# A new set of scheduling numbers for a two-layer decoder trunk on one NeuronCore

## The chip, the cores and the metric

The kernel runs on one core of one Trainium2 chip, in float32. The metric is the device time of one launch in microseconds (us). The engines of the core are named as in the profile: PE (matmuls; PEld its weight loads), DVE (the vector engine), ACT (the scalar engine), POOL (GpSimd) and SP (whose queue issues the DMAs here). All values are float32; products that need full precision are made of three matmuls, as described below.

## The reference

```python
for l in range(2):                                   # x: 256 tokens x 1024
    x = x + 0.5 * swiglu(rmsnorm(x, ffn1_norm[l]), ffn1_w_gate[l], ffn1_w_up[l], ffn1_w_down[l])
    h = rmsnorm(x, mix_norm[l])
    (q, kc, vc, ksl, vsl, kw, vw, gts, hq, hf, hi, hg) = split(h @ w_in[l])
    o_nsa = nsa_group(...)      # 8 heads of 64, 2 key groups: compressed, selected and window branches
    o_hg = hgrn2_group(...)     # 4 heads of 128: a gated linear recurrence in chunks of 64
    x = x + concat([o_nsa, o_hg]) @ w_out[l]
    x = x + 0.5 * swiglu(rmsnorm(x, ffn2_norm[l]), ffn2_w_gate[l], ffn2_w_up[l], ffn2_w_down[l])

def swiglu(x, w_gate, w_up, w_down):                 # w_gate, w_up: 1024 x 2816
    return (silu(x @ w_gate) * (x @ w_up)) @ w_down
```

So each layer is an FFN, a mixer (attention and recurrence side by side, one input and one output projection) and a second FFN.

## The kernel before

The 256 tokens stay in SBUF as two halves h = 0 and h = 1 of 128 rows (`X`). All weights are streamed once through the core in units of 128 x 1024 numbers: `load_stream` (L395) brings a unit into one of three raw buffers, `hi_stream` (L413, on ACT) rounds it to the high part `hi`, `lo_stream` (L432) takes the difference `lo = raw - hi` on DVE or, with `pool=True`, on POOL, and `stream(h)` (L458) multiplies: three matmuls per product, hi with the high part of the activations, lo with it, and hi with their low part (L485 to L487; `wide_unit`, L501, does the same with the weights as the moving operand at L515 to L517). The pairs hi, lo live in a ring of five slots; a raw buffer is free once `lo` is made, and a slot once both halves have used it.

The mixer's other work hangs on the blocks of the input projection, in the order q, kv, kw, hf, hq, hi, hg. `head_task` (L1166) makes the scores of two heads (matmuls L1174 and L1175), their row maxima and the exponentials; the weights of a head are then scaled by `buf<-buf,mx`, on DVE (L358) or ACT (L334). `turn_task` (L1194) transposes them, and `attend_task` (L1104) splits them into pth and ptl and multiplies with the values into the PSUM tile `po` (L1144 to L1146, L1158). `cmp_task` (L1203) does the branch of the compressed keys on tiles `pc`. The recurrence is in `level_task` (L1307): for chunks halved six times it forms `hx` from exponentials of the prefix sums `S` and `P`; `products` (L1348) multiplies these pieces on PE (L1368), `last_product` (L1378, matmul L1385) and the product `S<-S,kk` (at L1344, run by the helper `tt`, L345) close it, and `out_task` (L1400) makes the recurrence's output of each half in `po` (L1419 and L1421) and normalises it (squares on ACT into kk, sum at L1425, power on POOL, `kk<-po,ost`, which is the last reader of `po`). There is a single PSUM buffer `po`. Then the units of the output projection (`OUT_ORDER`, L1453: pairs of input part, 0 for attention and 1 for the recurrence, and output column half n) run through the same stream, `resid` (L672) adds x, `norm` (L680) normalises the rows (power on POOL at L376, scaling at L690) and `norm_turn` (L697) transposes the result for the next FFN (L382), whose stream needs it.

Nothing in this order is written out by hand. While the program is built, `Sched.run` (L212) holds all tasks that have a next operation ready to be placed, estimates for each the earliest start on each engine that may do it (`when`, L191, from the program's own cost formulas), picks the engine by the estimated end plus `BIAS` of that engine, and then the task with the smallest start plus its penalty. Penalties come from `PEN` by the name of the task, `STEP` by half or group, `PREP` for the two weight preparations by how far they are ahead, `FLOW` and `LAG` (`stream_pen`, L531) for the two streams, and `FIRST` for the first transposes. The result is one fixed list of instructions for each engine; the chip then runs each list in order, with semaphore waits between engines. Helpers that give the scheduler a choice of engine are `copy` (ACT or DVE), `tt` (DVE, and POOL where allowed) and `ts` (DVE, POOL or ACT). So the numbers set both the order and the engine.

Of the kernel before, what the change touches and what calls it, by code (L numbers as in the profile page):

```python
# [46 lines left out]
BOOT = 3  # L47

BOOT_X = ((-1, 0, 1, 2), (0, 0, 2, 4), (2, 1, 0, 2), (3, 1, 2, 4))
FIRST = (-0.3, -0.4, 0.5, 1.3, 0.1, 0.6, 0.9, 0.2)  # L50
LAG = 4
NBUF = 14
OUT_ORDER = ((0, 0), (0, 1), (1, 0), (1, 1))
POOL_LO = True
ORDER = ('q', 'kv', 'kw', 'hf', 'hq', 'hi', 'hg')

PEN = {"norm_turn": 0.1, "next_gain": 2.25, "gates_task": 0.15, "compress_task": -0.05, "level_task": 0.25,
       "boot": -1.0, "first_gain": -0.3, "first_norm": -0.25, "pad": 3.35, "hi_task": -3.8, "load_stream": 3.25,
       "done": 0.25, "kv_task": 0.65, "turn": 2.65, "load_w1": 3.15, "mix_prepare": -0.2, "c_turn": -3.3,
       "f_task": 0.25, "q_turn": 0.05, "kw_task": -6.1, "q_task": 0.6, "hg_task": 0.75, "hq_task": 0.45,  # L60
       "last_product": -0.15, "k_turn": 0.15, "products": 0.05, "turn_task": -0.1, "attend_task": -0.05,
       "out_task": 0.05, "k_task": 0.4, "cmp_task": -0.1, "first_turn": -0.65, "head_task": -0.1, "log_task": 0.15}
STEP = {'h': -0.16, 'g': 0.03, 'r': 0.0}
PREP = (-0.2, 0.25, 0.55, 0.75)
FLOW = (0.25, 0.15, 0.15)
BIAS = {'POOL': 0.1, 'ACT': -0.05}
SWITCH = 0.8


# [53 lines left out]
class Sched:  # L123
# [17 lines left out]
    def spawn(self, gen, pen=0.0, deps=(), phase=None):  # L141
        if not callable(pen):
            pen += PEN.get(gen.__name__, 0.0)
        t = Task(gen, pen, deps, phase)
# [61 lines left out]
            self.held[eng] = [x for x in mine if x[1] > low]  # L206
        self.held[eng].sort()

    def emit(self, t, eng, start, end, fn):
        fn()  # L210

    def run(self):  # L212
        while self.tasks:
            while any(not isinstance(t.req, Op) and self.resolve(t) for t in self.tasks):
                pass
            best = None
            for t in self.tasks:
                if not isinstance(t.req, Op):
                    continue
                pen = t.pen() if callable(t.pen) else t.pen  # L220
                one = None
                for eng, cost, fn, tab, port in t.req.alts:
                    start, more = self.when(t, eng, cost, port), 0.0
                    if eng == "PE" and (self.cold > 0 or start - self.free[eng] > 1.8):
                        cost *= 2
                    if tab and self.table not in tab:
                        cost, more = cost + LOAD, SWITCH
                    done = start + cost + BIAS.get(eng, 0.0)
                    if one is None or done < one[0]:
                        one = (done, start + pen + more, eng, start + cost, cost, fn, tab, port)  # L230
                if best is None or one[1] < best[0]:
                    best = (one[1], one, t)
            if best is None:
                if self.tasks:
                    raise RuntimeError("stuck: " + str([(t.gen.__name__, t.req[:2]) for t in self.tasks]))
                return
            _, (_, _, eng, end, cost, fn, tab, port), t = best
            if tab and self.table not in tab:
                self.table = tab[0]
                if tab[0] == "ln_exp":  # L240
                    self.nc.scalar.preload_act_table_set("natural_log_exp_and_others")
            self.emit(t, eng, end - cost, end, fn)
            if port:
                self.hold(eng, end - cost, end)
            if eng == "DMA":

                issued = end - cost + 0.475
                self.moved = max(issued + 0.65, self.moved) + cost
                end = self.moved + 0.87
            if eng == "PE":  # L250
                self.cold = (3.4 if end - cost - self.free[eng] > 1.8 else self.cold) - cost
            self.free[eng] = issued if eng == "DMA" else end
            t.deps = [(end, eng)]
            self.advance(t, (end, eng))
# [18 lines left out]
def wait(x):  # L273
    return ("wait", x)


def put(x):
    return ("set", x)
# [26 lines left out]
class Trunk(Sched):  # L305
# [148 lines left out]
    def prep_pen(self, which):  # L454
        lead = getattr(self, which) - max(self.at)
        return PREP[min(max(lead, 0), 3)]

# [73 lines left out]
    def stream_pen(self, h):  # L531
        p = min(self.phase_at[h], len(self.phases) - 1)
        a, b = self.phases[p]
        i, o = self.at[h], self.at[1 - h]
        if h and i >= b - LAG and o < b and p == self.phase_at[0]:
            return 2.0
        if not h and i < a + LAG and o >= a:
            return FLOW[0]
        return FLOW[1] + (FLOW[2] if i > o or (i == o and h) else 0.0)

# [320 lines left out]
    def mix(self, l):  # L861
# [69 lines left out]
        def values(h, br, src):  # L931

            c = lambda v: v[:, 2 * br + h, 64:].rearrange("p (g d) -> p g d", g=2)[:, :, :64]
            yield from self.split(c(M["vh"]), c(M["vl"]), src)
# [18 lines left out]
        def kw_task(h, ps):  # L953
# [7 lines left out]
            yield put(key("gt", h))  # L961
            sub(k_task(h), deps=self.keys[key("kr", h)], pen=STEP["h"] * h)
            sub(gates_task(h), deps=self.keys[key("gt", h)], pen=STEP["h"] * h)
            yield from values(h, 1, p3[:, 1])
# [139 lines left out]
        def attend_task(h, g):  # L1104
            for x in (("k", h), ("k", 0), ("q", h, g), ("g", h)):
                yield wait(key(*x))
            sub(cmp_task(h, g), pen=STEP["g"] * (2 * h + g))

# [15 lines left out]
            for r in range(R):  # L1124
                sub(head_task(h, g, r, part, pr, mx), deps=deps, pen=STEP["g"] * (2 * h + g) + STEP["r"] * r)
            for r in range(R):
# [6 lines left out]
            for i, (so, vi) in enumerate(tiles):  # L1133
                sub(turn_task(h, g, i, so, pr), deps=deps, pen=STEP["g"] * (2 * h + g) + STEP["r"] * i)
            for i, (so, vi) in enumerate(tiles):
# [316 lines left out]
        act = lambda h, kt: self.xact(h, kt) if kt > 3 else (M["ah", h][:, kt], M["al", h][:, kt])  # L1452
        for ni, (part, n) in enumerate(OUT_ORDER):  # L1453
            for k in (2 * part, 2 * part + 1):
                need = (lambda h, k=k: key("att", h, k)) if part == 0 else (lambda h: key("ho", h))
                first = k == 2 * part and part == OUT_ORDER[0][0]
                last = k == 2 * part + 1 and part == OUT_ORDER[-1][0]
                us.append(Unit(bs[n], 2 * k, [(wo[256 * k:256 * k + 256, 512 * n:512 * n + 512], 0)], first, last, act, need))

        def opened(pool, p):  # L1460
# [30 lines left out]
            for h in range(2):  # L1491
                for g in range(2):
                    sub(attend_task(h, g), pen=STEP["g"] * (2 * h + g))
                sub(log_task(h), pen=STEP["h"] * h)
# [8 lines left out]
    def build(self):  # L1503
# [12 lines left out]
        for h in range(2):  # L1516
            self.spawn(self.first_norm(h))
            for n in range(4):
                self.spawn(self.first_turn(h, n), pen=FIRST[4 * h + n])
        self.spawn(self.hi_stream(), pen=lambda: self.prep_pen("at_hi"))  # L1520
# [31 lines left out]
```

## Time and profile before

| | |
|---|---|
| runs | 1132.74, 1134.69 and 1187.89 us, median 1134.69 us |
| the profiled execution | 1132.6 us, of which the profile's span is 1130.8 us |
| PE | busy 1090.8 us (96%), mean granted clock 0.972 of full speed |
| DVE | busy 699.6 us (62%) |
| ACT | busy 577.1 us (51%) |
| POOL | busy 96.6 us (9%) |
| DMA | 186.16 MB, mean 165 GB/s |

The program's stages are seen in the span as follows: the first FFN up to about 208 us, the first mixer from 210 to about 392, two FFNs to 763, the second mixer from 765 to about 947, and the last FFN to the end. Busy times are sums over a stretch of the time in which an engine had an instruction running; an engine that is fully busy in a stretch sets its length, unless its clock is low there.

### The profile page before, as it was taken

Reading aid. Unit: us, or ns where it says so; the run is one execution under the profiler, and the core shown is the slowest. Engines: PE = TensorE matmul, PEld = TensorE weight load, DVE = VectorE, ACT = ScalarE, POOL = GpSimd, SP = SyncE. Lnnn points to the kernel's source line nnn. Section 1 sums busy time; section 2 is a strip of 40 time slices with the busy share of each in tenths; the row PEclk is TensorE's granted clock in tenths of the full one; section 3 lists DMA queues with packets and bytes.
Section 4 is the critical chain, followed back from the end, with each engine's and each line's share of the span. In section 5 each row is a group of like instructions: output and inputs, shape, how many; then the busy total and the mean of one; then the engine's idle time right before and its main releaser. Section 6 shows DMA issues by size and latency. Waiting matters only on the chain.

```text
span 1130.8 us, 18755 instructions
## 1 busy us (share of the span) xinstructions
PE 1090.8 (96%) x7420; PEld 975.9 (86%) x7420; DVE 699.6 (62%) x1242; ACT 577.1 (51%) x911; POOL 96.6 (9%) x124
## 2 busy tenths in 40 slices
PE   6999999999889999999999999999997899999998
PEld 4999988898668799998889999888975788999986
DVE  5665544689985755554465555448898857555543
ACT  6544444467664554443454444435866645444432
POOL 3100000041121100000010000001403201000000
PEclk9999999999879999999999999999998699999999
DMA  7666666565501476666666666556544125666553
GB/s 223 209 197 172 189 185 188 161 174 168 169 20 38 149 207 185 186 185 187 188 179 195 187 179 187 185 168 187 165 137 131 38 75 168 196 180 186 185 160 120
DMA packets 154168, 186.16 MB, mean 165 GB/s; under 512 B 7568, under 2 KB 117984, under 8 KB 154080
## 3 DMA queue, kind: packets, MB, share of 16 engines
q1 hardware_dynamic: 154080, 184.96, 55.1%
q8 instruction: 58, 0.95, 0.3%
q14 instruction: 30, 0.25, 0.1%
HBM read 183.89 MB, written 1.05 MB: 164 GB/s over the span
## 4 chain that ended last, share of the span: by engine, by line
PE 85%; DVE 9%; DMA 2%; issue 2%; ACT 1%; POOL 1%; SPq 0%; DVEq 0%; ACTq 0%; POOLq 0%
PE acc L515 15%; PE acc L516 15%; PE acc L517 15%; PE acc L485 11%; PE acc L487 11%; PE acc L486 11%; PE short L382 2%; DVE lo L347 2%; DVE buf L1178 1%; PE short L1368 1%; DVE xn L690 1%; DMA lg<-in_hgrn_lb_logits_dram 1%; DVE hx L347 1%; PE po L1146 1%; DVE buf L358 1%
## 5 line engine op out<-in xcount | busy, mean ns | idle before, releaser
L347 DVE TENSOR_TENSOR lo<-raw,hi 128x1024 fp32r<-128x1024 f32 (+2 forms) x329 | 394.9, 1202 | 287.2 <-ACT hi L334 286.0
L334 ACT ACTIVATE hi<-raw 128x1024 fp32r<-128x1024 f32 (+2 forms) x337 | 351.6, 1045 | 317.4 <-PE acc L487 108.0
L515 PE MATMUL acc<-xh,hi 128*128 128x256 f32 x1408 | 399.2, 284 | 0.0
L517 PE MATMUL acc<-xh,lo 128*128 128x256 f32 x1408 | 398.4, 283 | 0.0
L516 PE MATMUL acc<-xl,hi 128*128 128x256 f32 x1408 | 398.4, 283 | 0.0
L515 PEld LDWEIGHTS acc<-xh,hi 128*128 128x128 f32 x1408 | 270.2, 192 | 0.2
L516 PEld LDWEIGHTS acc<-xl,hi 128*128 128x128 f32 x1408 | 270.3, 192 | 0.1
L517 PEld LDWEIGHTS acc<-xh,lo 128*128 128x128 f32 x1408 | 270.2, 192 | 0.0
L485 PE MATMUL acc<-hi,th 128*128 128x512 f32 x352 | 139.7, 397 | 0.0
L486 PE MATMUL acc<-lo,th 128*128 128x512 f32 x352 | 139.2, 395 | 0.0
L487 PE MATMUL acc<-hi,tl 128*128 128x512 f32 x352 | 139.2, 395 | 0.0
L485 PE MATMUL acc<-hi,xh 128*128 128x512 f32 (+1 forms) x240 | 95.8, 399 | 0.0
L487 PE MATMUL acc<-hi,xl 128*128 128x512 f32 (+1 forms) x240 | 91.7, 382 | 0.0
L486 PE MATMUL acc<-lo,xh 128*128 128x512 f32 (+1 forms) x240 | 91.2, 380 | 0.0
L487 PEld LDWEIGHTS acc<-hi,tl 128*128 128x128 f32 x352 | 66.1, 188 | 16.1
L486 PEld LDWEIGHTS acc<-lo,th 128*128 128x128 f32 x352 | 66.2, 188 | 15.5
L485 PEld LDWEIGHTS acc<-hi,th 128*128 128x128 f32 x352 | 66.2, 188 | 15.5
L334 ACT ACTIVATE sg<-acc 128x512 f32<-128x512 f32 (+1 forms) x46 | 26.2, 570 | 72.0 <-PE acc L517 68.8
L376 POOL TENSOR_TENSOR rs<-rs,half 128x1 f32<-128x1 f32 x12 | 7.0, 587 | 572.6 <-DVE rs L683 572.6
L487 PEld LDWEIGHTS acc<-hi,xl 128*128 128x128 f32 x240 | 45.4, 189 | 9.1 <-DVE xl L347 0.4
L485 PEld LDWEIGHTS acc<-hi,xh 128*128 128x128 f32 x240 | 45.5, 190 | 7.8
L486 PEld LDWEIGHTS acc<-lo,xh 128*128 128x128 f32 x240 | 45.5, 190 | 6.9
(230 smaller groups left out, 1100.1 us busy)
## 6 DMA issues: line engine op xcount, KB each, us to landing
raw<-in_ffn_w_down_dram SPq DMA_DIRECT2D x88, 512.0 KB, 4.2
raw<-in_ffn_w_gate_dram SPq DMA_DIRECT2D x80, 512.0 KB, 3.8
raw<-in_ffn_w_up_dram SPq DMA_DIRECT2D x80, 512.0 KB, 3.9
raw<-in_w_in_dram SPq DMA_DIRECT2D x48, 512.0 KB, 3.8
raw<-in_w_out_dram SPq DMA_DIRECT2D x16, 512.0 KB, 3.7
buf<-in_cmp_w_dram SPq DMA_DIRECT2D x16, 256.0 KB, 7.3
raw<-in_ffn_w_gate_dram SPq DMA_DIRECT2D x13, 256.0 KB, 2.8
raw<-in_ffn_w_up_dram SPq DMA_DIRECT2D x13, 256.0 KB, 3.1
```

The costliest lines, as they stand in the source:

```text
L334: return ("ACT", c, lambda: self.nc.scalar.activation(out, in_, func, **k), TABLES.get(func), False)
L347: alts = [("DVE", 0.065 + 0.00104 * n, lambda: self.nc.vector.tensor_tensor(out, a, b, op), None, not in_psum(a) and not in_psum(b))]
L358: lambda: self.nc.vector.tensor_scalar(out, a, s1, s2, **k), None, not in_psum(a))]
L382: self.nc.tensor.transpose(o, i, self.ident[:i.shape[0], :i.shape[0]])
L485: f(ps[:, :k.n], ah, hi[:, t, :k.n], start=st, stop=False)
L486: f(ps[:, :k.n], ah, lo[:, t, :k.n], start=False, stop=False)
L487: f(ps[:, :k.n], al, hi[:, t, :k.n], start=False, stop=sp)
L515: f(ps[:, c], hi[:, t, j], xh, start=u.first and c == t == 0, stop=False)
L516: f(ps[:, c], hi[:, t, j], xl, start=False, stop=False)
L517: f(ps[:, c], lo[:, t, j], xh, start=False, stop=u.last and c == 1 and t == 3)
L690: toks.append((yield self.V(576, lambda: nc.vector.scalar_tensor_tensor(self.XN[h][:, c], self.X[h][:, c], rs[:, 0:1], self.gains[0][:, c] ...
L1146: f(po[:, :256], vh[:, vi, o:o + 128], tl[:, c], start=False, stop=False)
```

## The change

Only numbers are changed; the instructions that a task may ask for and all arithmetic stay. `emit`, an indirection around `fn()`, is taken out, so that from line 212 on a line stands three lower in the changed file. The core of the diff:

```diff
-FIRST = (-0.3, -0.4, 0.5, 1.3, 0.1, 0.6, 0.9, 0.2)
-LAG = 4
+FIRST = (-1.05, -1.18, 0.54, 0.89, 0.86, 0.63, 0.87, 0.46)
+LAG = 5
 NBUF = 14
-OUT_ORDER = ((0, 0), (0, 1), (1, 0), (1, 1))
+OUT_ORDER = ((0, 0), (0, 1), (1, 1), (1, 0))
...
-       "last_product": -0.15, "k_turn": 0.15, "products": 0.05, "turn_task": -0.1, "attend_task": -0.05,
-       "out_task": 0.05, "k_task": 0.4, "cmp_task": -0.1, "first_turn": -0.65, "head_task": -0.1, "log_task": 0.15}
-STEP = {'h': -0.16, 'g': 0.03, 'r': 0.0}
-PREP = (-0.2, 0.25, 0.55, 0.75)
-FLOW = (0.25, 0.15, 0.15)
-BIAS = {'POOL': 0.1, 'ACT': -0.05}
...
+       "k_turn": 0.16, "products": 0.15, "turn_task": -0.1, "attend_task": -0.03, "out_task": 0.06, "k_task": 0.42,
+       "cmp_task": -0.1, "first_turn": -0.74, "head_task": -0.1, "log_task": 0.16}
+STEP = {'h': -0.45, 'g': 0.03, 'r': 0.0}
+PREP = (-0.17, 0.21, 0.56, 0.75)
+FLOW = (0.16, 0.28, 0.46)
+BIAS = {'POOL': 0.07, 'ACT': -0.49}
```

`BIAS` is added to an operation's estimated end when the engine is chosen: ACT now takes one unless DVE would end more than 0.49 us earlier (0.05 before). `STEP['h']` is the lead that the second half's recurrence has over the first's, `FLOW` the penalty of the weight streams (the last number falls on the stream that is ahead of the other), and `OUT_ORDER` now leaves the column half n = 0 for the end.

In the order of the program this shows at many places of each mixer and at the start of the kernel; the FFNs' order in their steady part is the same as before. Three places follow.

The first is PE in the middle of the first mixer, where the stream has reached the third of the four hi units (`hi2`, `lo2` are ring slots, `xh` and `xl` the activations, `acc00` and `acc10` the two halves' sums). Before:

```order
L485 MATMUL acc00_63<-hi2_78,xh_84 128x512
L486 MATMUL acc00_63<-lo2_79,xh_84 128x512
L487 MATMUL acc00_63<-hi2_78,xl_85 128x512
L1368 MATMUL short1_68<-xn0_87,kk_1922 64x64 x8
...
L382 MATMUL short1_68<-ident_94,buf7_1895 128x128 x4
L485 MATMUL acc10_65<-hi2_78,xh_84 128x512
L486 MATMUL acc10_65<-lo2_79,xh_84 128x512
L487 MATMUL acc10_65<-hi2_78,xl_85 128x512
```

And now:

```order
L482 MATMUL acc00_63<-hi2_78,xh_84 128x512
L483 MATMUL acc00_63<-lo2_79,xh_84 128x512
L484 MATMUL acc00_63<-hi2_78,xl_85 128x512
L1171 MATMUL short0_67<-kh_1913,qs0_1924 128x256
L1172 MATMUL short0_67<-kl_1914,qs0_1924 128x256
L1171 MATMUL short1_68<-kh_1913,qs0_1924 128x256
L1172 MATMUL short1_68<-kl_1914,qs0_1924 128x256
...
L482 MATMUL acc10_65<-hi2_78,xh_84 128x512
```

Before, the recurrence's products (L1368) stood between the stream's matmuls and the heads' scores (L1174) came after all stream units of the input projection; now the first half's scores stand between the stream's matmuls, and the products (now L1365) come later, among the attention's transposes and value products.

The second is the end of the same mixer on PE, from the last value product of the compressed branch (`pct1`, `vcb`) on. Before (`acc00<-hi3,xh` is a unit of the output projection's part 1):

```order
L1158 MATMUL po_70<-pct1_1911,vcb_104 128x128 x2
L485 MATMUL acc00_63<-hi3_80,xh_84 128x512
...
L1419 MATMUL po_70<-xn1_91,S_1924 128x128
L1421 MATMUL po_70<-xn1_91,xn0_87 128x128
...
L485 MATMUL acc10_65<-hi0_74,ah1_1934 128x512
```

And now:

```order
L1155 MATMUL po_70<-pct1_1908,vcb_104 128x128 x2
L1365 MATMUL short1_68<-hx2_1901 64x32 x8
L1365 MATMUL short2_69<-hx0_1899 64x32 x8
L482 MATMUL acc00_63<-hi0_74,ah0_1922 128x512
...
L1382 MATMUL short0_67<-hx3_1902 64x64 x4
...
L1416 MATMUL po_70<-xn1_91,P_1920 128x128 x4
L1406 MATMUL short1_68<-P_1920,S_1921 128x128 x4
...
L1416 MATMUL po_70<-xn1_91,S_1921 128x128
L1418 MATMUL po_70<-xn1_91,xn0_87 128x128
```

Before, the first half's recurrence output (its `L1419 po<-xn1,P`, earlier than this piece) was made before the second half's attention had ended; now all attention is over when the last products of the recurrence run, and the two outputs (L1416, and L1416 with L1418) follow each other with nine stream matmuls between them.

The third is POOL in the first mixer. Before:

```order
L350 TENSOR_TENSOR hx3_1905<-hx3_1905,xn0_87 128x8x32
...
L350 TENSOR_TENSOR hx2_1904<-hx2_1904,kk_1922 128x4x64
L350 TENSOR_TENSOR lo2_79<-raw1_72,hi2_78 128x1024
L350 TENSOR_TENSOR P_1923<-P_1923 128x4x64
L1391 MEMSET P_1923 64x4x64
L350 TENSOR_TENSOR G0_1933<-G0_1933,og_115 128x512
```

And now:

```order
L347 TENSOR_TENSOR P_1920<-P_1920 128x8x32
L347 TENSOR_TENSOR S_1921<-S_1921,P_1920 128x256
L347 TENSOR_TENSOR P_1920<-P_1920 128x4x64
...
L347 TENSOR_TENSOR hx0_1899<-hx0_1899,kk_1919 128x8x32
L1388 MEMSET P_1920 64x4x64
L373 TENSOR_TENSOR ost0_1927<-ost0_1927,half_97 128x4
L373 TENSOR_TENSOR ost1_1936<-ost1_1936,half_97 128x4
L373 TENSOR_TENSOR rs0_89<-rs0_89,half_97 128x1
L347 TENSOR_TENSOR lo4_83<-raw2_73,hi4_82 128x1024
```

The unit `lo2<-raw1` in the middle of the mixer and most of the recurrence's pieces `hx` and `S` have left POOL for DVE; the unit `lo4<-raw2` behind the norm's power (`rs0`) is still on POOL, as it was before. Over the whole kernel DVE has 1213 instructions (1244 before), ACT 875 (825) and POOL 107 (126); PE has 7062 in both.

## Rows read from the trace of the kernel before

**Rows 1.** Windows: stretch, us, busy PE PEld DVE ACT POOL, PEclk, DMA share, GB/s.
```profile
60.00:200.00 140.00, 140.00 (x960) 130.00 (x960) 71.62 (x68) 61.70 (x70) 0.00 (x0) 1.00 0.63 188
260.25:345.86 85.61, 76.09 (x591) 59.37 (x590) 75.71 (x280) 57.95 (x152) 17.43 (x31) 0.84 0.37 112
265.00:297.00 32.00, 31.77 (x274) 23.90 (x273) 29.71 (x68) 19.22 (x37) 3.41 (x6) 1.00 0.47 145
297.00:350.00 53.00, 43.71 (x308) 34.60 (x307) 44.49 (x208) 37.10 (x117) 13.68 (x22) 0.74 0.26 78
345.86:377.57 31.71, 30.98 (x188) 26.66 (x187) 19.05 (x30) 14.70 (x25) 3.76 (x4) 1.00 0.24 73
815.03:900.52 85.49, 75.94 (x589) 58.66 (x587) 76.11 (x280) 58.00 (x152) 17.41 (x31) 0.84 0.36 111
```
**Rows 2.** Waits of DVE between 297 and 350: us in total, times, longest.
```profile
DVE ptl L347 <- ACT pth L334: 3.1, 4, 1.3
```
**Rows 3.** Timeline, first mixer, the recurrence's closing product: start, us, engine line operation.
```profile
345.17 0.69 DVE L347 TENSOR_TENSOR S<-S,kk 128x512 f32<-128x512 f32 x1
```
**Rows 4.** Groups by line and form, DVE and ACT: busy, mean ns, idle before.
```profile
L358 DVE TENSOR_SCALAR buf<-buf,mx 128x256 f32<-128x256 f32 x20 | 7.5, 384 | 0.0
L358 DVE TENSOR_SCALAR buf<-buf,mx 128x128 f32<-128x128 f32 x28 | 7.1, 281 | 0.0
...
L347 DVE TENSOR_TENSOR hx<-hx,kk 128x256 f32<-128x256 f32 x18 | 8.3, 458 | 0.0
L347 DVE TENSOR_TENSOR S<-S,P 128x256 f32<-128x256 f32 x20 | 8.4, 420 | 0.0
L347 DVE TENSOR_TENSOR lo<-raw,hi 128x1024 fp32r<-128x1024 f32 x315 | 385.1, 1224 | 287.2 <-ACT hi L334 286.0 <-DVE lvmask L817 0.2
L347 DVE TENSOR_TENSOR ptl<-short,pth 128x512 fp32r<-128x512 f32 x24 | 16.1, 688 | 9.9 <-ACT pth L334 9.9
...
L334 ACT ACTIVATE buf<-buf,mx 128x256 f32<-128x256 f32 x44 | 21.4, 499 | 9.9 <-DVE mx L347 7.7 <-DVE mx L358 1.7 <-POOL mx L360 0.4
```
**Rows 5.** Timeline, DVE operations beside POOL's weight splits in the first mixer.
```profile
330.89 0.23 DVE L347 TENSOR_TENSOR pc<-pc,mx 128x64 f32<-128x64 f32 x1
332.97 2.36 POOL L350 TENSOR_TENSOR lo<-raw,hi 128x1024 fp32r<-128x1024 f32 x1
333.26 2.14 DVE L347 TENSOR_TENSOR pc<-pc,mx 128x64 f32<-128x64 f32 x1
378.22 2.58 POOL L350 TENSOR_TENSOR lo<-raw,hi 128x1024 fp32r<-128x1024 f32 x1 [1.57 <-ACT hi L334]
378.48 2.86 DVE L690 SCALAR_TENSOR_TENSOR xn<-x,rs,gain 128x512 f32<-128x512 f32 x1
```
**Rows 6.** Timeline, end of the first mixer: recurrence outputs, stream matmuls, first transpose of `xn`.
```profile
350.81 0.39 PE L1419 MATMUL po<-xn,P 128*128 128x128 f32 x2
351.91 0.60 ACT L334 ACTIVATE kk<-po 128x512 f32<-128x512 f32 x1 [0.30 <-PE po L1419]
354.26 0.40 PE L487 MATMUL acc<-hi,al 128*128 128x512 f32 x1
354.57 0.69 DVE L347 TENSOR_TENSOR kk<-po,ost 128x512 f32<-128x512 f32 x1 [1.14 <-POOL ost L376]
354.96 0.39 PE L487 MATMUL acc<-hi,al 128*128 128x512 f32 x1
377.57 0.60 PE L382 MATMUL short<-ident,xn 128*128 128x128 f32 x4
```
**Rows 7.** Timeline, start of the kernel: a weight split on POOL, the norm, the first wide block.
```profile
16.78 2.40 POOL L350 TENSOR_TENSOR lo<-raw,hi 128x1024 fp32r<-128x1024 f32 x1
25.16 4.05 DVE L690 SCALAR_TENSOR_TENSOR xn<-x,rs,gain 128x512 f32<-128x512 f32 x4 [3.21 <-DMA gain<-in_ffn_norm_dram]
31.45 0.36 PE L515 MATMUL acc<-xh,hi 128*128 128x256 f32 x1
```
**Rows 8.** Windows, ten us in the middle of the mixer's attention.
```profile
320.00:330.00 10.00, 8.43 (x49) 6.68 (x51) 8.01 (x50) 8.03 (x30) 1.35 (x5) 0.54 0.01 2
```

More of the change, by code (lines that the diff above doesn't have):

```diff
@@ L49 @@
 BOOT_X = ((-1, 0, 1, 2), (0, 0, 2, 4), (2, 1, 0, 2), (3, 1, 2, 4))
-FIRST = (-0.3, -0.4, 0.5, 1.3, 0.1, 0.6, 0.9, 0.2)
-LAG = 4
+FIRST = (-1.05, -1.18, 0.54, 0.89, 0.86, 0.63, 0.87, 0.46)
+LAG = 5
 NBUF = 14
-OUT_ORDER = ((0, 0), (0, 1), (1, 0), (1, 1))
+OUT_ORDER = ((0, 0), (0, 1), (1, 1), (1, 0))
 POOL_LO = True
 ORDER = ('q', 'kv', 'kw', 'hf', 'hq', 'hi', 'hg')
[L57 to L60, printed above, removed]
-       "last_product": -0.15, "k_turn": 0.15, "products": 0.05, "turn_task": -0.1, "attend_task": -0.05,
-       "out_task": 0.05, "k_task": 0.4, "cmp_task": -0.1, "first_turn": -0.65, "head_task": -0.1, "log_task": 0.15}
-STEP = {'h': -0.16, 'g': 0.03, 'r': 0.0}
-PREP = (-0.2, 0.25, 0.55, 0.75)
-FLOW = (0.25, 0.15, 0.15)
-BIAS = {'POOL': 0.1, 'ACT': -0.05}
+PEN = {"norm_turn": 0.11, "next_gain": 1.21, "gates_task": 0.15, "compress_task": -0.05, "level_task": 0.33, "boot":
+       -1.4, "first_gain": -0.52, "first_norm": -0.26, "pad": 4.07, "hi_task": -1.73, "load_stream": 2.72, "done":
+       0.33, "kv_task": 0.75, "turn": 0.35, "load_w1": 2.96, "mix_prepare": 0.27, "c_turn": -3.76, "f_task": 0.01,
+       "q_turn": 0.26, "kw_task": -7.36, "q_task": 0.57, "hg_task": 0.73, "hq_task": 0.76, "last_product": -0.12,
+       "k_turn": 0.16, "products": 0.15, "turn_task": -0.1, "attend_task": -0.03, "out_task": 0.06, "k_task": 0.42,
[4 more added lines that the diff above has]
+BIAS = {'POOL': 0.07, 'ACT': -0.49}
 SWITCH = 0.8
@@ L207, in hold @@
         self.held[eng].sort()
-    def emit(self, t, eng, start, end, fn):
-        fn()
     def run(self):
@@ L241, in run @@
                     self.nc.scalar.preload_act_table_set("natural_log_exp_and_others")
-            self.emit(t, eng, end - cost, end, fn)
+            fn()
             if port:
```

## The prediction

> **What bounds the kernel now.** I read the windows by stage first. In an FFN's steady part PE is busy for the whole of a stretch (140 of 140 us) while DVE and ACT have half of it free [rows 1]: there the length is the matmuls' own, and since neither their number nor their order changes there, the four FFNs cost what they did. The two mixers differ. From the first mixer's last prefix sum, at 260.25, to the recurrence's closing product `S<-S,kk`, which ends at 345.86 [rows 3], DVE is busy 75.71 of 85.61 us (88.4%), PE 76.09 at a mean clock of 0.84, ACT 57.95 (68%) [rows 1]. In the first part of it (265 to 297) PE and DVE are both nearly full; from 297 to 350 no stream feeds PE, whose clock falls to 0.74, DVE has 84% and ACT 70% [rows 1]. The waits of DVE say the rest of the story there: the longest sum, 3.1 us, is for ACT's `pth` [rows 2]. So the middle of the mixer is paced by DVE, in a chain that goes back and forth between DVE, ACT and PE. Then, from 345.86 to the first transpose of the next norm at 377.57 [rows 6], PE is busy for 30.98 of 31.71 us at full clock [rows 1]: its own work sets the end. The second mixer repeats it (85.49 us, DVE 76.11) [rows 1]; I work out the first and double it.
>
> **Term 1, the middle of a mixer.** The same two points exist in the new order: the last `P<-P,S` and the product `S<-S,kk`. I count what DVE does between them, before and now, with the durations of before [rows 4].
> *Given to ACT:* the row scalings `buf<-buf,mx`, 7 of 128x256 at 0.384 and 7 of 128x128 at 0.281, together 4.66; and seven small copies of about 0.3 each (their form is nearest to the 0.281 row), 2.1. That is −6.8.
> *Taken from POOL:* five pieces `hx` at 0.458, three `S` at 0.420, one weight unit `lo` at 1.224 and one 128x512 product, which I price as the other of that size, 0.688. That is +5.5. One copy from ACT, +0.3.
> *Moved across the two ends:* the second half's attention now lies wholly ahead of the product, so six `ptl` at 0.688 and two more of 128x256 at about 0.42 come in (+5.0), while small softmax and key operations worth about 2.2 leave to the time before. That is +2.8.
> The sum is −6.8 + 5.5 + 0.3 + 2.8 = +1.8 in single durations. Neighbours on DVE overlap in the trace: 247 durations here sum to about 93.4 against 75.71 busy [rows 1], 0.07 each; there are ten instructions fewer now, so that 0.7 of overlap is lost, +2.5.
>
> Against this stands one gain that a count does not show. A DVE operation that meets a weight split on POOL lasts until the split ends: the `pc` product takes 2.14 us beside the POOL split of 2.36, and 0.23 undisturbed [rows 5], 1.9 lost; with three smaller meetings with POOL's `hx`, `S` and `P` pieces I find 4.2 us of such excess in the stretch (the smaller ones were read the same way, each against its undisturbed form). The `lo2` in the middle has left POOL, and of the recurrence's pieces few remain; I take 3.1 of the 4.2 as gone. DVE's work becomes 75.7 + 2.5 − 3.1 = 75.0 us.
>
> A rule bears on this: by the Trainium skill, "SBUF — State Buffer", section "Who interferes with whom", DVE and GpSimd share a port pair as a lock held for a whole instruction, and whoever comes second stands still. The trace agrees (2.14 against 0.23, ending with the split). It speaks against the change at one place, where `lo4` stays on POOL beside the norm's scaling.
>
> How long do 75.0 us of work take? The share of DVE in the new stretch is the open price. Bounds from rows: 93% (29.71 of 32, while ACT is at 60%) and, on the other side, 76%, which I estimate by going on from 93% at ACT 60% and 84% at ACT 70% to ACT at 79% [rows 1]. ACT takes over 14 scalings of up to 0.499 [rows 4] and the copies at about 0.36, some 9 us: 67 of about 89, 75%. I take 84%, the row in which ACT is nearest to that. 75.0 / 0.84 = 89.3, so the product ends at 349.5, 3.7 us *later* than before.
>
> **Term 2, the mixer's end.** What follows the product is shorter. Before: 377.57 − 345.86 = 31.7 us, in which value products of the second half's attention still stood. Now, on PE, with the stream's matmuls at 0.233 (0.70 for three, 354.26 to 354.96 [rows 6]): copies into `P` 1.4, the first recurrence output and the product beside it 1.8, nine stream matmuls 2.1, a wait of about 0.6 for the single `po`, the second output 1.8; then a transpose and 12 stream matmuls 3.2 with about 1.1 of waits, a transpose 0.4, and 18 + 21 stream matmuls 9.1. That is 21.4. The wait for `po` comes from the rows: from the squares' start at 351.91 to the end of `kk<-po,ost` at 355.26 are 3.35 us [rows 6], and the matmuls placed between cover the rest. What is late next is the transpose of the second half's output, queued before the last 39 matmuls; its wait is the 0.9 in the 1.1.
> The first transpose of `xn` then stands at 349.5 + 21.4 = 370.9 instead of 377.57: −6.7 a mixer. Bounds: with 93%, 340.9 + 21.4 = 362.3, −15.3; with 76%, 358.9 + 21.4 = 380.3, +2.8.
>
> **Term 3, from norm to FFN.** The scalings at L690 meet `lo4` on POOL before (2.86 against 2.58 of the split [rows 5]), and `lo4` is on POOL still. I price the passage at nothing, because both orders leave one such meeting and stream units of the next FFN stand ready on PE to cover it; without that cover it costs or saves 2.1 us a mixer (±4 for two).
> By the skill's rule above, the second to come stands still: if each passage newly held a scaling, the sum would be 4.2 us higher.
>
> **Term 4, the start.** The fourth weight unit's split goes from POOL (2.40 at 16.78) to DVE (1.22 [rows 4]). Its raw buffer comes free up to 2.1 us sooner, and behind it in SP's queue stands the DMA of the gain, for which DVE's first scalings wait 3.21 us until 25.16, and with them the first wide block at 31.45 [rows 7]. The transposes between are also regrouped. Nothing to −2.4; I take the middle, −1.2.
> Cost at nothing: the swap in `OUT_ORDER` and the order in the FFN stages, where PE is full either way.
>
> **The sum.** Against the profiled execution's 1132.6 us (span 1130.8 and 1.8 around it; the median of the runs is 2.1 higher): 1132.6 − 2 × 6.7 − 1.2 = **1118 us**.
>
> **The rivals.**
> *Better interleaving.* With the first half's scores among the hi units, PE has stream work while DVE and ACT exchange data, so DVE stays as busy as before (88.4%) or as full as at 265 to 297. Then 84.8 to 80.6 us, −11.1 to −15.3 a mixer: 1109 to 1101. For it: the waits [rows 2] are for results that would be there earlier. Against: ACT gets some 9 us more.
> *ACT as the pace.* The scalings now run on ACT at 0.499 instead of 0.384 [rows 4], and ACT already has the accumulating exponentials and `pth`, for which DVE waits [rows 2]. When DVE's share falls to 78% the gain is gone (75.0 / 0.782 = 95.9, all that Term 2 gives back): 1131 to 1137.
> *The clock, slower than before.* PE's granted clock is 0.54 between 320 and 330 [rows 8], so nearly all at the lower level, 1.2 of 2.4 GHz, in the stretch without stream units; from 345.86 on it is 1.00 [rows 1]. If the clock is still low when the last 60 stream matmuls begin, they take 0.466 instead of 0.233: +14.0 a mixer, 1118 + 28 = 1146. It decides when low clock reaches past the closing product. Against: stream units are now left for the middle.
> By the Trainium skill, "TensorE: Matmul & The Clock Gate", section "Part 1: The HAM clock gate", the clock follows how busy PE was recently; the rows here agree (0.54 in a thin stretch, 1.00 in a full one).
> *No effect where it counts* is within the second rival.
>
> **How the numbers follow.** Chances: forecast (1111 to 1127) 0.47, better interleaving 0.22, ACT as the pace 0.20, the clock 0.11. The range 1103 to 1136 leaves out the better part of the second case (0.06), the clock case and the tail of the third, some 0.19. About 2% can be told from no change in this kernel: the bounds are 1112.0 and 1157.4 around the median of 1134.69. Faster: the second case and a little of the first, 0.26. Slower: a clock case worse than costed, 0.03. The rest, 0.71.
>
> **What would show it.** Right: from the last `P<-P,S` to `S<-S,kk` some 89 us with DVE at 84% and ACT near 75%; then 21 us to the first transpose of `xn`; no `pc` or `hx` on DVE longer than 1 us; the first wide block before 31; 140 of 140 us in the FFNs. Wrong: DVE's waits for ACT grown by more than 6 us in that stretch; a clock below 1 after the product; the passage to the FFN longer by more than 2 us; or a product that ends before 345, which would mean that I undervalue the interleaving.

## The result and the profile after

The changed kernel takes 1096.57 us (median of four; 1094.74 to 1097.36) against 1133.72 us of the kernel before, measured beside it. One of the four runs of the kernel before, at 1187.89 us, fell in the chip's slower state and is left out of the ratio, which is 0.9682, 95% interval 0.965 to 0.9714: some 36 us less. The forecast was 1118 with a range of 1103 to 1136; the time is 6 us below the range's lower end. The profiled execution took 1094.74 us with a span of 1093.0.

The busy times over the whole span (engine, busy us, share, instructions):

```profile
PE 1065.2 (97%) x7420; PEld 961.5 (88%) x7420; DVE 681.6 (62%) x1211; ACT 590.5 (54%) x961; POOL 68.0 (6%) x105
```

PE is busy 25.6 us less than before with as many instructions, and its mean granted clock is 0.995 of full speed (0.972 before). The windows that answer to [rows 1] follow, with the columns as there: an FFN's steady part; the middle of the first mixer (again from the last `P<-P,S` to `S<-S,kk`), its stage of the hi units (265 to 297) and the rest of it; the end (from there to the first transpose of `xn`); and the middle of the second mixer:

```profile
60.00:200.00 140.00, 140.00 (x948) 129.47 (x948) 70.27 (x67) 59.85 (x67) 0.00 (x0) 1.00 0.64 188
257.66:337.06 79.40, 75.45 (x667) 63.18 (x666) 74.21 (x275) 67.95 (x180) 7.69 (x22) 0.96 0.43 126
265.00:297.00 32.00, 31.55 (x226) 25.36 (x225) 29.35 (x152) 29.70 (x96) 1.77 (x8) 1.00 0.54 152
297.00:337.06 40.06, 36.56 (x388) 30.98 (x387) 37.77 (x109) 32.58 (x76) 5.30 (x11) 0.91 0.26 80
337.06:359.72 22.66, 21.33 (x113) 17.39 (x112) 15.15 (x22) 10.83 (x18) 3.29 (x4) 1.00 0.31 93
794.09:873.78 79.69, 74.66 (x667) 62.31 (x666) 74.41 (x275) 67.92 (x180) 7.67 (x22) 0.98 0.42 125
```

The FFNs are as they were. The middle of the first mixer ends at 337.06, well ahead of the 345 that the prediction had named as the sign of an undervalued interleaving. The middle of the mixer is 79.4 us instead of 85.6, and in it DVE is busy 93% of the time and ACT 86%. The row to look at longest is that from 265 to 297: PE and DVE were nearly full there before, too, but ACT had 19.22 of 32 us to do; now it has 29.70, in the same time and with the other two as full as they were. Reading the same points in both traces gives a ledger of the 37.8 us by which the profiled span is shorter, in us per place (first mixer and second where there are two; the forecast is per mixer):

| place | before | after | change | forecast |
|---|---|---|---|---|
| start, to the first transpose of `xn` at the first mixer | 207.99 | 204.99 | −3.0 | −1.2 |
| from there to the last `P<-P,S` | 52.3, 52.5 | 52.7, 52.7 | +0.4, +0.2 | 0 |
| middle, to the end of `S<-S,kk` | 85.6, 85.5 | 79.4, 79.7 | −6.2, −5.8 | +3.7 |
| end, to the first transpose of `xn` | 31.7, 31.7 | 22.7, 22.7 | −9.0, −9.0 | −10.3 |
| passage, to the last transpose of `xn` | 12.6, 11.0 | 9.1, 9.1 | −3.5, −1.9 | 0 |

The FFNs between these points differ by 0.3 us at most.

### The profile page after: what moved, and what is told of

Its sections match the earlier page's. It is cut to its first block, busy times and chain, and to the rows that moved or that the text cites. A ratio compares the mean times of both kernels' runs of the same rounds, so it can differ in the third digit from the quotient of the medians.

```text
span 1093.0 us, 18731 instructions
## 1 busy us (share of the span) xinstructions
PE 1065.2 (97%) x7420; PEld 961.5 (88%) x7420; DVE 681.6 (62%) x1211; ACT 590.5 (54%) x961; POOL 68.0 (6%) x105
## 4 chain that ended last, share of the span: by engine, by line
PE 83%; DVE 8%; ACT 4%; DMA 2%; issue 1%; SPq 1%; POOL 0%; DVEq 0%; ACTq 0%; POOLq 0%
PE acc L513 15%; PE acc L512 15%; PE acc L514 14%; PE acc L482 11%; PE acc L483 11%; PE acc L484 11%; PE short L379 2%; DVE lo L344 2%; ACT buf L331 1%; ACT hi L331 1%; DMA raw<-in_w_in_dram 1%; PE short L1365 1%; DVE xn L687 1%; DMA buf<-in_cmp_w_dram 1%; DMA gain<-in_ffn_norm_dram 1%
## 5 line engine op out<-in xcount | busy, mean ns | idle before, releaser
L344 DVE TENSOR_TENSOR lo<-raw,hi 128x1024 fp32r<-128x1024 f32 (+2 forms) x334 | 400.6, 1202 | 282.2 <-ACT hi L331 281.2
L331 ACT ACTIVATE hi<-raw 128x1024 fp32r<-128x1024 f32 (+1 forms) x336 | 350.7, 1045 | 308.5 <-PE acc L484 108.0
L331 ACT ACTIVATE sg<-acc 128x512 f32<-128x512 f32 (+1 forms) x46 | 26.1, 568 | 74.0 <-PE acc L514 66.6
L344 DVE TENSOR_TENSOR sg<-acc,sg 128x512 f32<-128x512 f32 (+1 forms) x46 | 30.2, 657 | 33.6 <-PE acc L514 28.9
```

The costliest lines, as they stand in the source:

```text
L331: return ("ACT", c, lambda: self.nc.scalar.activation(out, in_, func, **k), TABLES.get(func), False)
L344: alts = [("DVE", 0.065 + 0.00104 * n, lambda: self.nc.vector.tensor_tensor(out, a, b, op), None, not in_psum(a) and not in_psum(b))]
```

## The experiments

Some kernels change numbers of the planner. In others the planner's choice is replaced by a recorded list: each of the 4103 operations is named by its task and its place in the task, with the engine it is to run on, and is placed in the order of the list. With its own list a kernel keeps every engine's sequence of instructions (the traces of the two runs with added load, below, have it but for the added ones); with another, order and engine can be changed one without the other. The two kernels differ in the engine of 127 operations. The core of that edit, cut:

```diff
-                    if one is None or done < one[0]:
-                        one = (done, start + pen + more, eng, start + cost, cost, fn, tab, port)
+            want, eng = self.picks.pop(0)
+            t = next(t for t in self.tasks if t.lab == want and isinstance(t.req, Op))
```

Line numbers in those kernels stand about 70 higher. The lists are too long to print: where a diff below has `picks`, `undo`, `more` or `rank`, it says in short what the list holds.

**Order against engines.** The first four runs ask whether the order or the lighter DVE made the gain.

```diff
-FLOW = (0.25, 0.15, 0.15)
+FLOW = (0.16, 0.28, 0.46)
```

> The kernel before with one line changed, FLOW = (0.16, 0.28, 0.46). In its order the first half's scores stand among the hi units, as in the changed kernel, while the engine choices follow the old BIAS. Theory 1 (interleaving: DVE's share in the middle rose to 93% because independent work of the stream, the heads and the recurrence stands side by side): most of the 38 us is there, 1100 to 1108, with DVE at 90% or more of its stretch and PE's clock at 0.95 or more there. Theory 2 (relief: the work given to ACT and taken from POOL is what shortens the chain on DVE): less than 12 us, 1122 or more, DVE's share near 88%.

Measured: 1111.95 us, ratio 0.984 (0.9814 to 0.9866), 18.6 us less than before, between the two theories and nearer the first. One line of the planner gives half of the gain. What theory 1 said of the middle came as stated: DVE is busy for 96% of it, with ACT at 77% and PE's clock at 0.95.

```profile
262.60:345.45 82.85, 75.53 (x668) 62.75 (x667) 79.67 (x287) 64.06 (x165) 11.49 (x26) 0.95 0.44 133
```

```diff
-BIAS = {'POOL': 0.1, 'ACT': -0.05}
+BIAS = {'POOL': 0.07, 'ACT': -0.49}
```

> The kernel before with one line changed, BIAS = {'POOL': 0.07, 'ACT': -0.49}. ACT takes the row scalings and copies; the scores still come after all stream units. Theory 1 (interleaving): within 6 us of the kernel before, 1127 to 1139, clock in the middle still below 0.9. Theory 2 (relief of DVE): at least half of the 38 us, 1115 or less.

Measured: 1126.76 us, ratio 0.9968 (0.9952 to 0.9984). This line by itself is worth 4 us, as theory 1 said. It moves some of the order as well: the mixer's end takes 28.8 us in this kernel instead of 31.7.

The order of the changed kernel on the old engines:

```diff
-    picks = [(op, engine_after(op)) for op in order_after]
+    picks = [(op, engine_before(op)) for op in order_after]
```

> The order in which the changed kernel places its 4103 operations, each on the engine that the kernel before gives it (127 operations differ in engine). Theory 1 (interleaving): at least 70% of the gain, 1107 or less, clock in the middle 0.95 or more. Theory 2 (relief): at most 30% of it, 1122 or more.

Measured: 1117.46 us, ratio 0.9885 (0.9859 to 0.9912): a third of the gain, which neither theory gave. And the old order on the new engines:

```diff
-    picks = [(op, engine_before(op)) for op in order_before]
+    picks = [(op, engine_after(op)) for op in order_before]
```

> The order in which the kernel before places its 4103 operations, each on the engine that the changed kernel gives it. Theory 1 (interleaving): at most 30% of the gain, 1122 to 1136, clock in the middle still near 0.84. Theory 2 (relief): 1115 or less. The splits that leave POOL alone should give about 4 us by the port waits of 1.9 us and more that I counted.

Measured: 1131.15 us, ratio 0.9999 (0.9983 to 1.0015): nothing. The 4 us that were expected of the port waits did not show. Order alone −13, engines alone 0, both −36: they work through each other. The windows show where. Middle and end of the first mixer with the new order on old engines:

```profile
265.58:351.10 85.52, 74.75 (x651) 60.64 (x650) 76.80 (x286) 62.10 (x158) 17.57 (x30) 0.96 0.38 113
351.10:374.02 22.92, 21.65 (x112) 17.54 (x113) 16.04 (x24) 10.71 (x17) 4.75 (x6) 1.00 0.30 92
```

The order alone gives the whole shortening of the end (22.9 instead of 31.7), and its middle, which has taken in that work, is as long as before. What the new engines add in this order, by the same ledger, is 6 us a mixer in the middle, 3 us a mixer in the stage ahead of it and 5 us at the start. The chain of waits fits this: its pieces over the middle lie on DVE for 46.8 of 85.5 us in the new order on old engines, and for 37.9 of 85.6 in the kernel before, so DVE is where relief can be felt in the new order. And the old order on new engines, the hi stage (265 to 297), the attention stage behind it (297 to 350), and the whole middle:

```profile
265.00:297.00 32.00, 31.63 (x272) 23.62 (x271) 28.30 (x62) 20.98 (x40) 3.24 (x4) 1.00 0.45 143
297.00:350.00 53.00, 42.79 (x314) 33.91 (x315) 43.15 (x203) 42.41 (x134) 4.66 (x13) 0.77 0.27 80
260.61:345.49 84.88, 74.30 (x588) 57.68 (x588) 72.35 (x268) 64.56 (x172) 10.16 (x22) 0.86 0.37 113
```

Here ACT is still free in the hi stage (20.98 of 32), and the scalings given to it land in the attention stage, where it goes from 37.10 [rows 1] to 42.41 while DVE has hardly less to do (43.15 for 44.49). Over the whole middle DVE is at 85% and ACT at 76%: in the old order one finds nearly the share that the prediction assumed, 84% with ACT at 75%. The chain of waits says the same. Its shares by line over the middle, cut at the right, in the kernel before and with the new engines in its order:

```profile
by line: DVE buf L1178 7.5%; PE acc L485 7.3%; DVE lo L347 6.4%; PE short L1368 6.2%; PE acc L487 5.9%; PE acc L486 5.9%; PE short L382 5.8%; DVE hx L347 3.7%; DVE buf L358 3.5%; DVE P L347 3.0%; PE short L1215 2.8%; DVE pc L347 2.7%; PE po
by line: ACT buf L402 11.7%; PE acc L553 10.1%; PE acc L554 7.8%; PE acc L555 7.8%; PE short L1436 7.5%; DVE lo L415 6.6%; DVE buf L1246 4.6%; PE short L450 4.5%; issue 4.0%; DVE buf L415 3.5%; DVE ptl L415 3.1%; DVE hx L415 2.4%; DVE S L41
```

The scalings left the chain on DVE (`buf L358`, 3.5%, 3.0 us) and came back into it on ACT: `ACT buf L402`, 11.7%, holds exponentials too, but 3.3 us of it are scalings. My reading is that in an order in which the next thing waits for the scaled row anyway, it doesn't matter who is spared.

**Is DVE full?** The next runs started from the idea (theory W) that DVE's work divided by 0.93 is the length of the new middle. Both keep the changed kernel's order.

```diff
+    undo = lambda op: {engine_before(op), engine_after(op)} == {"DVE", "ACT"}
-    picks = [(op, engine_after(op)) for op in order_after]
+    picks = [(op, (engine_before if undo(op) else engine_after)(op)) for op in order_after]
```

> The changed kernel's order and engines, except that the 61 operations which the change moved between DVE and ACT are back on the engine they had before; those that left or joined POOL stay moved. In the new order DVE was busy for 89.8% (order alone) to 93.4% of the middle, so I now take it for saturated there. Theory W (work on DVE over 0.93): DVE's work rises by about 7 us a mixer, the time by about 2 x 7.5 to 1108 to 1114. Theory L (what counts is that chains no longer pass through the slow POOL or wait for its port): within 5 us of the changed kernel, below 1102.

The list undoes 66 operations (the texts put on record for this run and the next have the two counts, 61 and 66, exchanged). Measured: 1109.74 us, ratio 0.9805 (0.9778 to 0.9833), 13 us slower than the changed kernel, as W said; in the first mixer's middle DVE has 4.2 us more (W had 7 for the mixer) and the middle is 4.7 us longer. Some 6 of the 15.5 us between the profiled spans lie ahead of the two middles.

```diff
+    undo = lambda op: engine_before(op) != engine_after(op) and "POOL" in (engine_before(op), engine_after(op))
```

> The changed kernel's order and engines, except that the 66 operations which left POOL or joined it are back on the engine they had before; the work given to ACT stays there. Theory W (work on DVE over 0.93): the pieces leave DVE again, 5 us a mixer, and some 4 us of port waits come back, so the time stays within 4 us of the changed kernel, 1093 to 1101. Theory L (latency and port of POOL): 1104 or more, with DVE's operations on hx, S and pc beside POOL's stretched to over 1 us and DVE's share of the middle below 90%.

Measured: 1107.2 us, ratio 0.9781 (0.9754 to 0.9808), 10.6 us slower than the changed kernel, above W's range and in L's. But the ledger puts 5.9 us of it at the start, where POOL makes a weight split again, and about 3 us a mixer in the middle, though DVE has less to do there (73.07 us, 88% of it). Without the start the run would lie between the two theories, so it speaks against W less clearly than its time does. First mixer, these two kernels:

```profile
262.14:346.20 84.06, 74.62 (x645) 60.72 (x644) 78.38 (x294) 62.19 (x160) 7.80 (x22) 0.96 0.37 114
263.52:346.12 82.60, 75.52 (x666) 62.69 (x666) 73.07 (x266) 68.39 (x178) 16.65 (x30) 0.96 0.40 121
```

Then the other direction, more of DVE's work to ACT:

```diff
+    more = lambda op: op is a row scaling of head_task and engine_after(op) == "DVE"
+    picks = [(op, "ACT" if more(op) else engine_after(op)) for op in order_after]
```

> The changed kernel's order and engines, except that the 20 row scalings which DVE still makes (ten a mixer) go to ACT too. Theory W (DVE's work over 0.93 sets the middle): 3.1 us less on DVE, 3.3 a mixer, 1089 to 1091. Theory A (ACT, at 86% of the middle, becomes the pace when it gets 4.4 us more, 91%): 1095 or more, with DVE's share below 91%.

Measured: 1098.27 us, ratio 0.9711 (0.9694 to 0.9729), not faster than the changed kernel, as theory A said. The middle is 81.33 us with DVE at 90% and ACT at 87%:

```profile
257.88:339.21 81.33, 75.60 (x667) 62.13 (x666) 73.15 (x265) 70.81 (x190) 7.68 (x22) 0.98 0.41 123
```

With 78.4, 74.2 and 73.2 us on DVE and 62.2, 68.0 and 70.8 on ACT the middle takes 84.1, 79.4 and 81.3: of these three splits the changed kernel's gives the shortest middle.

Finally, load added on DVE in both orders, eight row sums of 0.66 us a mixer behind the heads' reciprocals:

```diff
+                if self.heads % 2:
+                    nc.vector.tensor_reduce(self.scr1, self.con[:, 0:512], AX.X, OP.add)
```

> The kernel before, its order and engines, with eight row sums of 512 columns added on DVE in each mixer, one behind every second head's reciprocal; each takes 0.6 to 0.7 us, about 5.3 a mixer, and its result is not used. Theory W (in this order DVE has slack in the attention stage, the chain through ACT and PE sets its length): less than half of it is seen, the kernel slower by at most 5 us. If DVE is the pace in this order too: slower by 9 to 12 us.

> The changed kernel, its order and engines, with the same eight row sums a mixer behind the same heads. Theory W (DVE is full in the new middle): all of it is seen, slower by 9 to 12 us, 1106 to 1109. If DVE has slack here too: slower by at most 5 us.

Measured: 1138.92 us in the old order, ratio 1.0066 (1.0048 to 1.0084), 7.2 us for 10.6 us of work; in the new order 1102.34 us, ratio 0.9742 (0.9727 to 0.9757), which is 5.8 us over the changed kernel. Two middles, old order and new, with the load:

```profile
261.79:350.83 89.04, 77.84 (x590) 60.77 (x590) 80.42 (x288) 58.45 (x152) 17.35 (x31) 0.81 0.36 107
257.59:340.65 83.06, 76.03 (x667) 63.11 (x666) 78.61 (x283) 68.69 (x180) 7.68 (x22) 0.96 0.40 121
```

Both theories fell here: DVE is not slack in the old order, nor is it the sole limit in the new one. Which order takes in the added work better is not shown, since 7.2 and 5.8 us lie within each other's noise. A higher busy share of DVE is not a sign that DVE alone sets the pace.

**FLOW and BIAS together**, on the kernel before (the two lines shown above):

> The kernel before with two lines changed, FLOW and BIAS. Alone FLOW gave 1112 (-19 us) and BIAS 1127 (-4). If relief of DVE pays only where the order lets DVE be full (theory W), BIAS is worth more on top of FLOW than alone: 9 us or more, 1095 to 1103. If the two are independent: 1108.

Measured: 1113.96 us, ratio 0.9847 (0.9829 to 0.9865), no better than FLOW alone, and slower than either theory had it. The ledger shows a gain that is paid back: against FLOW alone the middles are 1.8 and 1.2 us shorter, and the stages ahead of them 1.9 and 1.8 us longer. So these two lines don't make the changed kernel's gain; the rest of it comes with the order that the whole set makes.

**The clock.** The kernel before, with 41 idle matmuls a mixer in the gaps of PE:

```diff
+                for _ in range(int((gap - 0.1) / 0.24)):
+                    self.nc.tensor.matmul(ps, self.XH[:, 0, 0:128], self.XH[:, 0:2], start=True, stop=True)
```

> The kernel before, in its own order, with 82 idle matmuls of 512 columns added on PE (41 a mixer, 9.6 us at full clock) wherever the planner left PE a gap in the attention stage; they write to a sum buffer that is free and is overwritten later. Theory C (the low clock, 0.5 to 0.7 of full speed in that stage, is what stretches the chain there): the clock in the middle rises to 0.93 or more and the middle gets shorter by 4 us or more a mixer, the kernel faster by 8 to 16 us. Theory E (the low clock is an effect of the waiting and costs little by itself, since the middle is paced by DVE and the chain through ACT): clock up all the same, the middle within 2 us of 85.6, the time within 5 us of the kernel before or slower.

Measured: 1129.62 us, ratio 0.9985 (0.9968 to 1.0002). The middles of the two mixers:

```profile
260.23:345.93 85.70, 80.52 (x633) 62.55 (x633) 76.47 (x281) 58.98 (x154) 18.23 (x31) 0.92 0.38 114
813.65:896.64 82.99, 76.38 (x624) 58.13 (x623) 76.44 (x281) 59.14 (x154) 18.09 (x31) 0.98 0.39 115
```

The clock is up to 0.92 and 0.98 (0.84 before), and the middle is no shorter in the one and 2.5 us shorter in the other. So theory E, nearly: raising the clock in this way gained nothing that shows in the kernel's time. It is a net result, for the fillers stand in PE's queue themselves: 36 in each middle, 13.5 and 12.2 us of PE's time, and in 13 of 24 places the program's next matmul followed right behind the last of them. What the low clock of [rows 8] would cost without them no run shows.

**Port waits.** Weight splits taken off POOL, in the new order (five) and in the old one (ten):

```diff
-            yield self.tt(lo[:, :, :n], r[:, :, :n], hi[:, :, :n].bitcast(F32), OP.subtract, pool=POOL_LO)
+            yield self.tt(lo[:, :, :n], r[:, :, :n], hi[:, :, :n].bitcast(F32), OP.subtract)
```

(as engines of the recorded lists, so that the order stays.)

> The changed kernel's order, with the five weight splits that POOL still makes put on DVE. At the passage from mixer to FFN the scaling that takes 2.28 us beside such a split should take 0.75, and PE's wait of 1.33 us for it should go: 1.3 us a mixer, 2 to 4 us in all, 1093 to 1095. If POOL's splits were relief for DVE there, the time stays within 1 us or rises.

> The kernel before, its order and engines, with its ten weight splits on POOL put on DVE. My count of port waits says: 1.9 us (the pc product) and 2.1 us (the norm's scaling) a mixer go, 1.2 us of splitting comes to DVE for each, so 2 to 5 us less in all, and up to 2 us at the start; 1124 to 1129. If the waits were covered or the splits on POOL were worth as much: within 1.5 us.

Measured: new order 1096.13 us, ratio 0.9688 (0.9664 to 0.9712), where the changed kernel has 0.9682; old order 1130.89 us, ratio 0.9996 (0.9984 to 1.0008). Nothing in either, though the stretched operations are gone. In the old order this is a sum: the middles are 1.8 and 0.5 us shorter (83.81 and 85.02) and the start 1.8 us longer; a split that leaves POOL costs DVE 1.22 us [rows 4]. The scalings behind the first mixer, new order without the split:

```profile
359.04 0.75 DVE L756 SCALAR_TENSOR_TENSOR xn<-x,rs,gain 128x512 f32<-128x512 f32 x1
...
360.30 0.74 DVE L756 SCALAR_TENSOR_TENSOR xn<-x,rs,gain 128x512 f32<-128x512 f32 x1
```

(2.28 for the second in the changed kernel.) The passage shrank only from 9.1 to 8.6 us, since PE then waits 0.8 us for the other half's scaling.

**The swap in OUT_ORDER**, undone in the changed kernel:

```diff
-OUT_ORDER = ((0, 0), (0, 1), (1, 1), (1, 0))
+OUT_ORDER = ((0, 0), (0, 1), (1, 0), (1, 1))
```

> The changed kernel with OUT_ORDER as before. PE's order in the mixer stays as it is but for which column half the last units of the output projection fill. I costed this swap at nothing: within 1.5 us of 1096.6. If the swap shortened the passage from mixer to FFN (12.6 and 11.0 us before, 9.1 now): 1098.5 or more.

Measured: 1096.39 us, ratio 0.9695 (0.9671 to 0.9719). The swap has no effect that can be seen, as expected.

**Only the heads' place undone:**

```diff
+    rank[op] = max(rank[op], rank_of_last_hg_unit)      # for the first half's head_task alone
```

> The changed kernel's order and engines, with one thing undone: in each mixer the 16 operations chains of the first half's scores (the eight heads' score matmuls and what hangs on them) may start only when all eight hi and hg units have passed through PE, as in the kernel before; everything else keeps its rank. Theory I (the gain of the middle and of the end comes from heads and stream standing side by side): at least 20 of the 36 us are lost, 1116 or more, clock in the middle back below 0.9, DVE and ACT both lower in share. Theory J (it comes from the rest of the order, the engines and the end of the mixer): 1106 or less.

Measured: 1208.97 us, ratio 1.0692 (1.0656 to 1.0728). It is far slower than the kernel before, so this run doesn't tell the two theories apart by size: with the heads gone nothing stands beside the stream, since the recurrence's products, which stood there before, come later in this order. From 265 to 297 and from 297 to 385:

```profile
265.00:297.00 32.00, 26.10 (x171) 21.19 (x169) 17.89 (x47) 12.45 (x20) 0.00 (x0) 0.98 0.64 192
297.00:385.00 88.00, 49.44 (x354) 36.98 (x355) 46.88 (x194) 47.85 (x142) 5.50 (x15) 0.62 0.08 25
```

It shows what it costs when neither heads nor recurrence stand beside the stream: ACT is busy 12.45 and DVE 17.89 of 32 us, and then come 88 us in which no engine is busy much over half of the time. What the heads' place alone is worth it can't show.

## Why the prediction was wrong

The loads were forecast well and the length was not. Point by point:

*What bounds the kernel.* "Paced by DVE" was half of it. In the kernel before, the pieces of the chain of waits over the first mixer's middle add up to 43.5 us on PE, 37.9 on DVE and 2.3 on ACT; in the changed kernel to 30.6, 26.1 and 15.2, and 4.6 for a weight's DMA. The middle is a chain through all three engines, and the load added on DVE showed in either order, but only in part.

*Term 1, the failed step.* DVE's work in the middle was put at 75.0 us and measured at 74.2 and 74.4; ACT's at 67 and measured at 68.0. What failed is the sentence "I take 84%, the row in which ACT is nearest to that": the share came out at 93%. It rested on two stretches of the kernel before in which DVE's share fell as ACT's rose, 93% at 60% and 84% at 70%. That was no law but two different stages. In the first ACT had little to do because no heads were there; in the second there was hardly any stream beside the attention, whose steps wait for one another. The runs show that the share hangs on the order and not on ACT's share alone: with the new engines DVE is at 85% of the middle in the old order and at 93% in the new one (88% and 90% with the old engines), and with ACT at nearly the 75% of the forecast it is at 85% in one kernel (old order, new engines; ACT 76%) and at 96% in another (the FLOW run; ACT 77%). The new order puts the first half's heads, with ACT's exponentials and scalings, into the stage where ACT had been free 40% of the time, and the three engines are then busy for 92 to 99% of it. With 93.4% for 84% the forecast's own sum would have given 80.3 us for the middle and −15.6 a mixer, 1100 us. The 93% stood among the forecast's bounds, at −15.3 a mixer or 1101 us, and the range began above it, at 1103. What takes the measured time below even that are Terms 3 and 4.

*The port waits in Term 1.* The stall is real in the row (2.14 us against 0.23) and gone with the split (0.22), but taking the splits off POOL left the kernel's time in the old order where it was, with gains of 1.8 and 0.5 us in the middles and a loss at the start. No run shows what the 3.1 us a mixer taken as gone are worth in the new order by themselves.

*Term 2* was right in kind, and its gain 1.3 us a mixer too large (the end takes 22.7 us where 21.4 were forecast).

*Term 3* was put at nothing and was −3.5 and −1.9. About 0.5 is the shorter wait for the scaling (1.33 instead of 1.84 us), 1.4 are six stream matmuls that now stand elsewhere, and in the first mixer some 1.5 the clock, which was 0.86 in the passage before and is 1.00 now.

*Term 4* was −3.0 for −1.2. The gain's DMA is issued at 17.38 instead of 19.63, 2.25 us sooner, as forecast (2.1); the first wide block starts at 29.52 instead of 31.45 [rows 7]. So the saving was near the whole of the 2.1 us, where I had taken half. The other 1.1 us lie behind that block: all 16 transposes of `xn` stand ahead of it now (12 before), and a wait of PE of 0.57 us for a DMA, at 42.8 before, is gone.

*Readings.* In the kernel before, some stream matmuls do stand between 330 and 350, where I wrote that no stream feeds PE; DVE has five instructions fewer in the new middle, not ten; and 75.7 + 2.5 − 3.1 is 75.1. None of these moves the forecast by as much as 1 us a mixer.

*OUT_ORDER at nothing* was right, as far as the noise lets one see.

*The rivals.* "Better interleaving" was the one that happened, and its mechanism, results that are there earlier because stream, heads and recurrence stand side by side, is borne out by the FLOW run (half of the gain from it alone); the late heads fit it but took the recurrence's products from the stream as well. I gave it 0.22, held against it that ACT gets 9 us more, and that was the error: ACT had room in the new place. "ACT as the pace" is not far away: 2.9 us more on ACT in the middle, and the kernel is no faster. The clock rival went the other way, clock up; the filler run found no gain from a higher clock, net of the fillers' own time.

What stays open: which of the other numbers (the task penalties, STEP, PREP) bring the 15 us beyond FLOW. FLOW's kernel has the same end (22.8 us) and loses against the changed one in the middle (82.9 and 82.1 us), at the start (209.3) and in the passage, and BIAS on top of it didn't help; no run took the others one by one. Open, too, is how much the heads' place alone brings.

## What to carry to other kernels

When an order moves work to another stage, add up each engine's work in that stage and ask who had room there, and don't carry a busy share over from a stage whose chain was different. A choice of engines and an order have to be judged together: here one gave 13 us, the other nothing, and both 36. A stretched instruction is not yet a loss of that size: here the kernels took as long without the stretched ones as with them.

## What the runs showed of the hardware

PE's granted clock and the time parted ways: with filler matmuls, which took PE's time themselves, the clock in the middle rose from 0.84 to 0.92 and 0.98, and the kernel's time changed by 0.15%, which is within the noise. And a single wait of 1.84 us of PE, the same in both mixers of the kernel before, stood in a passage with a mean clock of 0.86 in the one (part of it at the lower level) and 1.00 in the other:

```profile
381.40 0.66 PE L382 MATMUL short<-ident,xn 128*128 128x128 f32 x4 [1.84 <-DVE xn L690]
936.07 0.66 PE L382 MATMUL short<-ident,xn 128*128 128x128 f32 x4 [1.84 <-DVE xn L690]
377.57:390.12 12.55, 10.71 (x47) 8.42 (x47) 10.59 (x12) 5.72 (x10) 3.14 (x2) 0.86 0.49 143
932.23:943.25 11.02, 9.18 (x46) 7.17 (x46) 10.17 (x12) 5.72 (x10) 3.14 (x2) 1.00 0.53 148
```

The order of the two passages is the same, so these 1.5 us were not to be forecast from the order alone.
